# A two-layer hybrid block on one core: the causal mask goes beside the maximum, work moves from VectorE to ScalarE, and the first and last stages are written in another order

## The chip, the core and the metric

The kernel runs on one core of a Trainium2 chip. The core has a matmul engine (TensorE, PE in the profile, with its weight loads as PEld), a vector engine (VectorE, DVE), a scalar engine (ScalarE, ACT), a small general engine (GpSimd, POOL) and SyncE (SP), which issues most of the DMAs. Each engine works through its own list of instructions in order and waits on semaphores of the others. Matmul results land in PSUM; DVE and ACT take them from there to SBUF. The metric is the device time of one execution in microseconds (us); lower is better.

## The reference

512 tokens of width 1024 go through two layers, each a mixing part and a gated feed-forward part, with RMS norms before and after each and a residual sum. Layer A mixes by chunked spatial gating, layer B by attention with forget gates over 12 heads of 64 (the "fox" heads here). Both add four heads of attention over 256 memory rows. Cut to what the change touches:

```
def forgetting_attention(q, k, v, log_f):
    c = jnp.cumsum(log_f, axis=1)
    ...
        logits = jnp.einsum('bthd,bshd->bhts', qi, k).astype(jnp.float32) * scale
        logits = logits + ci[..., :, None] - cT[..., None, :]
        mask = kpos[None, :] <= qpos[:, None]
        logits = jnp.where(mask, logits, -jnp.inf)
        p = jax.nn.softmax(logits, axis=-1).astype(v.dtype)
        return jnp.einsum('bhts,bshd->bthd', p, v)

    # end of each layer
    f = (jax.nn.silu(f @ w_ffn_gate[layer]) * (f @ w_ffn_up[layer])) @ w_ffn_down[layer]
    h = h + rmsnorm(f, ln_ffn_post[layer])
```

where `rmsnorm(x, g)` is `x * rsqrt(mean(x * x) + 1e-6) * g` along the width.

## The kernel before

The state `h` is kept transposed in SBUF: 8 blocks of 128 rows of the width, by 512 tokens (`h`, 128x8x512). Every fp32 operand of a product is cut into two parts, `hi` and `lo` (`split`, L241: ACT casts the high part, DVE subtracts to get the low part), and `mm3` (L193 to L195) makes three matmuls of each product: hi by hi, lo by hi, hi by lo. Weights stream from HBM in pieces of 512 KB through four `raw` buffers (SP issues them) and are split on the way. So PE always has three matmuls for one product, while ACT and DVE split the next weights beside it. The order of the work is that of the code, except that the framework's scheduler may move instructions past each other on each engine; the order listings below show what came out.

**Start (`layer_a`).** `query_weights(m, c0, c1)` loads and splits a piece of the two blocks of query weights, `tokens(k0, k1)` loads blocks of the input into `h` and splits them scaled by the norm's gain (`ahi` L245 on ACT, `alo` L246 on DVE). The first products then run over k, both query blocks for each k, and behind each of the two products of k = 0 stand two matmuls on zeros (`idle`, L88), which only keep PE busy. Then follow the value blocks (`v`), the norm's sums, and the rest of the layer.

**Spatial gating of layer A.** `spatial(g)` makes two PSUM tiles `s` from the ring of three buffers named `lg` (the rings are `mm` and `lg` with three buffers each, `tr` with two). Just before, two tiles `rows` of the same ring are filled, and DVE adds them into `bsp` (L768).

**Fox heads of layer B (`attend`, `FoxHead`, `Softmax`).** For each head there are four blocks of 128 queries, `tb` = 3, 2, 1, 0, that see 512, 384, 256 and 128 keys. `steps` fixes the order of one head: S3, S2, S1, S0 are the logits, N2 and N0 the scalings, T0 to T2 the transposes and V0 to V2 the value products of the head before, and F0 to F4 pieces of other work (key, value and output blocks). One step S (`logits`) makes two matmuls into a PSUM tile `lg` (L504, L505) and a third (L506) that adds the causal mask: -1e30 above the diagonal, as a bf16 128x128 product of `neg` with an identity, `ident_b`. `weigh` then takes the row maximum on DVE (L440, `nmx`) and the exponential on ACT from PSUM into `p` in SBUF, with the row's sum `sm` (L441). `norm` inverts two sums and scales two blocks of `p` on DVE (L448, L450). `turn` transposes `p` on PE (L457) into `tr` and splits it (`pT`), and `values` multiplies it with the values (L525). `value_block` in `layer_b` takes 12 blocks of values, 128x256, out of PSUM on DVE, scaled by the norm (L1247).

**End (`tail_of`, `give`).** The last feed-forward product is made for four blocks of 128 tokens, `tail(0)` to `tail(3)`. Each gives two PSUM tiles `y` of 128x512, which DVE adds to the sums so far (L816); ACT takes the sums of squares (L819), POOL the power -1/2 (L262), and ACT scales the rows by it (L840; in the last block L836 on ACT and L835 on DVE). In the last block the second tile is made in two halves of 256 columns, in one PSUM tile. `give(tb, ...)` transposes the finished rows back, 128x128 at a time (`turned`, L847), and `residual` (L852) multiplies each transposed block with the gain and adds it to `h`, one DVE instruction for each 128x128. Then `h` goes out by DMA (L1369). Between the last product and the last transposes eight matmuls on zeros keep PE busy.

## Time and profile before

| | before |
|---|---|
| median of 3 runs | 1113.27 us (1113.27 to 1113.5) |
| the profiled execution's own time | 1111.68 us |
| its span, first to last instruction | 1110.0 us |
| PE busy | 1100.9 us, 7384 matmuls |
| PEld busy | 999.7 us |
| DVE busy | 895.0 us |
| ACT busy | 667.1 us |
| mean granted clock of PE | 0.999 |

Times are microseconds from the start of the span. In a row of a timeline stand the start, the length, the engine, the line of the kernel, the operation, the tiles written and read, and in brackets how long the engine was idle before and what ended that. Matmuls are pipelined, so their lengths overlap; what one costs is the distance from its start to the next one's start. A row of a table by groups shows count, busy time, mean ns of one, and idle time before them. A row of a table by windows shows the stretch, its length, and the busy time of PE, PEld, DVE, ACT and POOL in it (with counts), the granted clock, the share of the DMA engines, and GB/s. What the profile calls ACTIVATION_READ_ACCUMULATOR is a second instruction, by which ACT writes out a row sum.

### The profile page before, as it was taken

To read this page: it belongs to the slowest core of one execution; us is meant where nothing else is said; L and a number is where in the kernel's file an instruction comes from. 1 tells how busy PE (TensorE), PEld (TensorE's weight loads), DVE (VectorE), ACT (ScalarE), POOL (GpSimd) and SP (SyncE) were. 2 spreads that over 40 slices of the span, in tenths; PEclk is the share of its full clock that TensorE was granted. 3 is DMA by queue.
4 is the path that set the end of the run, shared out by engine and by line. 5 is a ranking of instruction groups with operands and counts; after the bars stand their busy time and mean duration, and the time that the engine had idled before them with its cause. 6 is when DMAs were issued, how large, how long until landed. Compare 5 with 4: busy or idle time off the path is not lost.

```text
span 1110.0 us, 19527 instructions
## 1 busy us (share of the span) xinstructions
PE 1100.9 (99%) x7384; PEld 999.7 (90%) x7385; DVE 895.0 (81%) x1734; ACT 667.1 (60%) x1401; POOL 25.1 (2%) x41
## 2 busy tenths in 40 slices
PE   9999999999999999999999999999999999999998
PEld 6997889999899899998988897889999899899996
DVE  7879659897698598787868889868897698588775
ACT  7776578664366254477647667768665266254453
POOL 0000000000000000001000000000000000000000
PEclk9999999999999999999999999999999999999999
DMA  7521331334135133245222555431234134233222
GB/s 268 159 79 58 113 116 39 115 115 136 55 115 152 56 96 115 79 150 173 77 76 75 155 124 131 129 115 39 77 97 151 58 115 134 58 114 114 77 76 77
DMA packets 63558, 118.13 MB, mean 106 GB/s; under 512 B 5164, under 2 KB 39992, under 8 KB 63464
## 3 DMA queue, kind: packets, MB, share of 16 engines
q1 hardware_dynamic: 62584, 116.05, 34.4%
q8 instruction: 58, 0.95, 0.4%
q0 software_dynamic: 192, 0.52, 0.2%
q10 hardware_dynamic: 688, 0.31, 0.1%
q14 instruction: 36, 0.29, 0.1%
HBM read 104.71 MB, written 2.10 MB: 96 GB/s over the span
## 4 chain that ended last, share of the span: by engine, by line
PE 86%; DVE 3%; ACT 1%; issue 1%; DMA 0%; POOLq 0%; POOL 0%; DVEq 0%; ACTq 0%
PE y L193 10%; PE y L194 10%; PE y L195 10%; PE a L194 5%; PE a L195 5%; PE a L193 5%; PE ps L193 3%; PE ps L194 3%; PE ps L195 3%; PE x L194 3%; PE x L195 3%; PE x L193 3%; PE e L193 3%; PE e L194 3%; PE e L195 3%; PE tr L457 1%
## 5 line engine op out<-in xcount | busy, mean ns | idle before, releaser
L241 ACT CAST whi<-raw 128x512 fp32r<-128x512 f32 x460 | 277.2, 620 | 266.6 <-PE y L195 118.5
L241 DVE TENSOR_TENSOR wlo<-raw,whi 128x512 fp32r<-128x512 f32 x460 | 306.3, 686 | 117.0 <-ACT whi L241 114.6
L193 PE MATMUL y<-whi,fhi 128*128 128x512 f32 (+1 forms) x356 | 139.7, 393 | 0.0
L194 PE MATMUL y<-wlo,fhi 128*128 128x512 f32 (+1 forms) x356 | 139.5, 392 | 0.0
L195 PE MATMUL y<-whi,flo 128*128 128x512 f32 (+1 forms) x356 | 139.1, 391 | 0.0
L194 PE MATMUL x<-xslo,whi 128*128 128x256 f32 x320 | 89.9, 281 | 0.0
L194 PE MATMUL a<-xslo,whi 128*128 128x256 f32 x320 | 89.9, 281 | 0.0
L195 PE MATMUL x<-xshi,wlo 128*128 128x256 f32 x320 | 89.8, 280 | 0.0
L193 PE MATMUL x<-xshi,whi 128*128 128x256 f32 x320 | 89.7, 280 | 0.0
L195 PE MATMUL a<-xshi,wlo 128*128 128x256 f32 x320 | 89.7, 281 | 0.0
L193 PE MATMUL a<-xshi,whi 128*128 128x256 f32 x320 | 89.6, 280 | 0.0
L195 PEld LDWEIGHTS y<-whi,flo 128*128 128x128 f32 x356 | 66.9, 188 | 15.5 <-DVE flo L241 0.2
L193 PEld LDWEIGHTS y<-whi,fhi 128*128 128x128 f32 x356 | 66.9, 188 | 15.1 <-DVE y L816 0.2
L194 PEld LDWEIGHTS y<-wlo,fhi 128*128 128x128 f32 x356 | 66.9, 188 | 14.7 <-DVE wlo L241 0.2
L193 PE MATMUL ps<-xshi,whi 128*128 128x256 f32 (+1 forms) x224 | 68.4, 306 | 0.0
L194 PE MATMUL ps<-xslo,whi 128*128 128x256 f32 (+1 forms) x224 | 66.7, 298 | 0.0
L195 PE MATMUL ps<-xshi,wlo 128*128 128x256 f32 (+1 forms) x224 | 66.4, 298 | 0.0
L193 PEld LDWEIGHTS a<-xshi,whi 128*128 128x128 f32 x320 | 60.3, 189 | 0.4
L194 PEld LDWEIGHTS a<-xslo,whi 128*128 128x128 f32 x320 | 60.2, 188 | 0.3
L193 PEld LDWEIGHTS x<-xshi,whi 128*128 128x128 f32 x320 | 60.3, 188 | 0.0
L195 PEld LDWEIGHTS x<-xshi,wlo 128*128 128x128 f32 x320 | 60.2, 188 | 0.0
L194 PEld LDWEIGHTS x<-xslo,whi 128*128 128x128 f32 x320 | 60.2, 188 | 0.0
(289 smaller groups left out, 3082.1 us busy)
## 6 DMA issues: line engine op xcount, KB each, us to landing
raw<-in_w_gate SPq DMA_DIRECT2D x44, 512.0 KB
raw<-in_w_up SPq DMA_DIRECT2D x44, 512.0 KB
raw<-in_w_down SPq DMA_DIRECT2D x44, 512.0 KB
raw<-in_w_out SPq DMA_DIRECT2D x16, 512.0 KB
raw<-in_w_b_q SPq DMA_DIRECT2D x8, 512.0 KB
raw<-in_w_a_v SPq DMA_DIRECT2D x6, 512.0 KB
raw<-in_w_a_u SPq DMA_DIRECT2D x6, 512.0 KB
raw<-in_w_v SPq DMA_DIRECT2D x6, 512.0 KB
```

The source lines that it names most:

```text
L193: PE.matmul(o, w[0], x[0], start=start, stop=False, skip_group_check=more)
L194: PE.matmul(o, w[0], x[1], start=False, stop=False, skip_group_check=more)
L195: return PE.matmul(o, w[1], x[0], start=False, stop=stop, skip_group_check=more)
L241: last_parts[:] = A.copy(hi, src), (eng or V).tensor_sub(lo, src, hi)
L457: PE.transpose(tr[:, at * P : (at + 1) * P], src, ident)
```

## The change

1. **Mask.** The third matmul and `ident_b` go. `neg` becomes 128x512 in bf16, zero but for its last 128 columns. DVE's maximum becomes one `tensor_tensor_reduce`: it adds the last `n` columns of `neg` to the logits, takes the negative, writes the result to `p` in SBUF and reduces by the minimum to `nmx`. In the listing that is two instructions, named ISA: the operation, and the write of `nmx`. The exponential then works in place on `p`, with scale -1.
2. **Scaling.** For the widest block of each head (`tb` = 3, 512 columns) ACT scales `p` instead of DVE (`by_scalar`).
3. **Values.** ACT takes layer B's 12 value blocks out of PSUM instead of DVE.
4. **Start.** The tokens' blocks 0 to 3 are loaded one by one ahead of the second query block's first half; the second halves come later; the first products run by halves of k, one query block after the other, and the four matmuls on zeros are gone.
5. **Spatial gating.** The two tiles `s` come from the rings `mm` and `lg` in turn.
6. **End.** The last norm's gain is turned to a row on PE, written to HBM (a tile `row`, issued by ACT) in layer A and read back into a `raw` buffer, 128x1024, the same row in every partition, behind `tail(0)`. For the last two blocks of tokens DVE multiplies the sums with the gains ahead of the norm (`gained`), so that the transposed blocks are only added to `h`, 256 or 512 columns at a time. The last block's second half has a PSUM tile of its own. The transposes of block 2 stand behind the last product, and six matmuls on zeros instead of eight behind them.

```diff
-    ident_b = cp.tile([P, P], BF16, name="ident_b")
-    V.tensor_copy(ident_b, ident)
...
-    neg = cp.tile([P, P], BF16, name="neg")
-    V.tensor_copy(neg, neg_f[:, :P])
+    neg = cp.tile([P, T], BF16, name="neg")
+    V.tensor_copy(neg, neg_f)
...
-        def weigh(self, tb, lg, p):
+        def weigh(self, tb, lg, p, mask=None):
...
+            else:
+                V.tensor_tensor_reduce(out=p, in0=lg, in1=mask, scale=-1.0, scalar=-NEG, op0=ALU.add, op1=ALU.min,
+                                       accum_out=self.nmx[:, c])
+                last_exp[0] = A.activation(p, p, AF.Exp, bias=self.nmx[:, c], scale=-1.0, accum_out=self.sm[:, c])
...
-                V.tensor_scalar_mul(self.p[x], self.p[x], self.sm[:, x : x + 1])
+                if x in self.by_scalar:
+                    A.activation(self.p[x], self.p[x], AF.Copy, scale=self.sm[:, x : x + 1])
+                else:
+                    V.tensor_scalar_mul(self.p[x], self.p[x], self.sm[:, x : x + 1])
...
-            PE.matmul(lg[:, :n], qc[:68, c], kc[:68, :n], start=False, stop=False)
-            PE.matmul(lg[:, c], ident_b, neg, start=False, stop=True)
+            PE.matmul(lg[:, :n], qc[:68, c], kc[:68, :n], start=False, stop=True)
...
+    def row_of_gains(block):
+
+        gain_row[0] = dp.tile([KT, P], F32, name="row")
+        o, row = ps("tr", (KT, P), s="gr"), temp("row", (KT, P))
+        PE.transpose(o, gains[:, block * KT : block * KT + KT], ident)
+        A.copy(row, o)
+        nc.scalar.dma_start(gain_row[0], row)
+
+    def spread_gains():
+
+        row = gain_row[0]
+        gain_row[0] = wp.tile([P, D], F32, tag="raw", name=name("raw"), bufs=4)
+        nc.sync.dma_start(gain_row[0], row.rearrange("a b -> (a b)").partition_broadcast(P))
...
         query_weights(0, 0, 512)
-        tokens(0, 1)
-        query_weights(1, 0, 1024)
-        tokens(1, 2)
-        tokens(2, 4)
+        for k in range(4):
+            tokens(k, k + 1)
+        query_weights(1, 0, 512)
         query_weights(0, 512, 1024)
         tokens(4, 6)
         tokens(6, 8)
         last_a = tuple(last_parts)
+        query_weights(1, 512, 1024)
...
-            for k in range(KT):
+            for half in range(0, KT, 4):
                 for o, w in zip(outs, wq):
-                    end = mm3(o, w[k], a[k], k == 0, k == KT - 1)
-                    if k == 0:
-                        idle(2, zero, end)
+                    for k in range(half, half + 4):
+                        mm3(o, w[k], a[k], k == 0, k == KT - 1)
...
-                    o = ps("lg", (P, 2, 2, P), s="s")
+                    o = ps(("mm", "lg")[tp2], (P, 2, 2, P), s="s")
...
+                    if added and not (final and dh):
+                        V.tensor_mul(gained[tb][dh][:, cols], y, gain_row[0][:, 512 * dh + m0 * P : 512 * dh + m1 * P])
...
-                    V.tensor_scalar_mul(ys[tb][1][:, cols], ys[tb][1][:, cols], r[:, c])
-                    A.activation(ys[tb][0][:, cols], ys[tb][0][:, cols], AF.Copy, scale=r[:, c])
+                    y0, y1 = (y[:, cols] for y in gained[tb])
+                    V.scalar_tensor_tensor(out=y1, in0=ys[tb][1][:, cols], scalar=r[:, c],
+                                           in1=gain_row[0][:, 512 + m * P : 512 + (m + 2) * P],
+                                           op0=ALU.mult, op1=ALU.mult)
+                    A.activation(y0, y0, AF.Copy, scale=r[:, c])
...
-                    V.tensor_scalar_mul(vals[j, tk // 2][:, tk % 2, :], o[tk][:, :256], r4b[:, tk : tk + 1])
+                    A.activation(vals[j, tk // 2][:, tk % 2, :], o[tk][:, :256], AF.Copy, scale=r4b[:, tk : tk + 1])
...
+    def give_added(tb, order, tags, queues=(nc.sync,), end=None, held={}):
...
+                for x, k in enumerate(some):
+                    row_turned(gained[tb], k, tr[:, x, :])
+            with behind(held.get(n, ())):
+                V.tensor_add(h[:, k0:k1, c[0] : c[1]], tr, h[:, k0:k1, c[0] : c[1]])
+            queues[n % len(queues)].dma_start(out[:, k0:k1, c[0] : c[1]], h[:, k0:k1, c[0] : c[1]])
...
-    idle(8, zero, end)
-    give(TB - 1, (range(4, 6), range(2), range(6, 8), range(2, 4)), (nc.sync, nc.scalar))
+    give_added(TB - 2, (range(2), range(2, 4), range(4, 8)), ("tr", "tr", "mm"), end=end, held={2: [sums]})
+    idle(6, zero, end)
+    give_added(TB - 1, (range(4, 6), range(2), range(6, 8), range(2, 4)), ("lg", "mm") * 2, (nc.sync, nc.scalar))
```

How the change stands in the lists of the engines is shown at three places. First PE in the middle of a fox head, at S3 (`lg`, from `ka` and `qa`, then `kc` and `qc`), with the transposes T1 of the head before (`tr`) behind it. Before:

```order
L504 MATMUL lg_7758<-ka_7659,qa_7658 128x512
L505 MATMUL lg_7758<-kc_6910,qc_6908 128x512
L506 LDWEIGHTS ident_b
L506 MATMUL lg_7758<-neg,ident_b 128x128
L457 MATMUL tr_7775<-ident,p_7682 128x128
L457 MATMUL tr_7775<-ident,p_7655 128x128
L457 MATMUL tr_7775<-ident,p_7631 128x128 x2
L504 MATMUL lg_7784<-ka_7659,qa_7658 128x384
```

The same place now:

```order
L512 MATMUL lg_7752<-ka_7655,qa_7654 128x512
L513 MATMUL lg_7752<-kc_6912,qc_6910 128x512
L464 MATMUL tr_7768<-ident,p_7677 128x128
L464 MATMUL tr_7768<-ident,p_7651 128x128
L464 MATMUL tr_7768<-ident,p_7628 128x128 x2
L512 MATMUL lg_7777<-ka_7655,qa_7654 128x384
```

The mask's weight load and matmul are gone, 48 times in all; the rest of the heads' work on PE keeps its order but for a few places where neighbours changed.

Second DVE in the same head, from the low part of T0's transposes to the scaling of the two wide blocks (`nmx` is the negative maximum, `p` the weights, `sm` their sums). Before:

```order
L241 TENSOR_TENSOR pT_7751<-tr_7749,pT_7750 128x512
L440 TENSOR_REDUCE nmx_6928<-lg_7758 128x1
L241 TENSOR_TENSOR pT_7777<-tr_7775,pT_7776 128x512
L440 TENSOR_REDUCE nmx_6928<-lg_7784 128x1
L241 TENSOR_TENSOR wlo_7895<-q_6121,whi_7894 128x512
L440 TENSOR_REDUCE nmx_6928<-lg_7801 128x1
L448 RECIPROCAL sm_6929<-sm_6929 128x2
L241 TENSOR_TENSOR pT_7813<-tr_7811,pT_7812 128x256
L450 TENSOR_SCALAR p_7762<-p_7762,sm_6929 128x512
L450 TENSOR_SCALAR p_7788<-p_7788,sm_6929 128x384
```

The same place now:

```order
L239 TENSOR_TENSOR pT_7745<-tr_7743,pT_7744 128x512
L443 ISA p_7755,nmx_6930<-lg_7752,neg 128x512
L443 ISA nmx_6930 128x1
L239 TENSOR_TENSOR pT_7770<-tr_7768,pT_7769 128x512
L443 ISA p_7780,nmx_6930<-lg_7777,neg 128x384
L443 ISA nmx_6930 128x1
L239 TENSOR_TENSOR wlo_7884<-q_6123,whi_7883 128x512
L443 ISA p_7796,nmx_6930<-lg_7793,neg 128x256
L443 ISA nmx_6930 128x1
L452 RECIPROCAL sm_6931<-sm_6931 128x2
L239 TENSOR_TENSOR pT_7804<-tr_7802,pT_7803 128x256
L457 TENSOR_SCALAR p_7780<-p_7780,sm_6931 128x384
```

Each maximum has become two instructions, the second of them one column wide; the scaling of 512 columns has left DVE, and on ACT it now stands between the exponential of 256 columns and that of 128.

Third DVE at the very end, from the sum of the last block's first half-tile on (`y` the sums, `yt` the transposed blocks, `two` and `v` the sums of squares, `r` the factor of the norm). Before:

```order
L816 TENSOR_TENSOR y_9720<-y_13392,y_9720 128x256
L852 SCALAR_TENSOR_TENSOR h<-yt_13440,gains,h 128x128 x2
L821 SCALAR_TENSOR_TENSOR v_13182<-ss_13181,two_13375,eps_13177 128x1
L852 SCALAR_TENSOR_TENSOR h<-yt_13440,gains,h 128x128
L835 TENSOR_SCALAR y_9720<-y_9720,r_13183 128x256 x2
L852 SCALAR_TENSOR_TENSOR h<-yt_13440,gains,h 128x128
L852 SCALAR_TENSOR_TENSOR h<-yt_13459,gains,h 128x128 x2
L852 SCALAR_TENSOR_TENSOR h<-yt_13465,gains,h 128x128 x2
L852 SCALAR_TENSOR_TENSOR h<-yt_13471,gains,h 128x128 x2
L852 SCALAR_TENSOR_TENSOR h<-yt_13477,gains,h 128x128 x2
```

The same place now:

```order
L841 TENSOR_TENSOR y_9674<-y_13372,y_9674 128x256
L1403 TENSOR_TENSOR h<-yt_13394,h 128x2x128
L1403 TENSOR_TENSOR h<-yt_13399,h 128x2x128
L848 SCALAR_TENSOR_TENSOR v_13136<-ss_13135,two_13337,eps_13131 128x1
L1403 TENSOR_TENSOR h<-yt_13404,h 128x4x128
L863 SCALAR_TENSOR_TENSOR yg_13336<-y_9674,r_13137,raw_13217 128x256 x2
L1403 TENSOR_TENSOR h<-yt_13423,h 128x2x128
L1403 TENSOR_TENSOR h<-yt_13418,h 128x2x128
L1403 TENSOR_TENSOR h<-yt_13428,h 128x2x128
L1403 TENSOR_TENSOR h<-yt_13433,h 128x2x128
```

Behind the last two products with `r` stand four sums of 256 columns where eight of 128 stood; ahead of `v` stand two sums of block 2.

More of the change, by code (lines that the diff above doesn't have):

```diff
@@ L430, in hybrid @@
     class Softmax:
+        by_scalar = ()
         def __init__(self):
@@ L511, in logits @@
             at = 384 if tb == 0 else 0
-            self.weigh(tb, lg[:, :n], (self.beside if tb == 0 else self.room)[:, at : at + n])
+            self.weigh(tb, lg[:, :n], (self.beside if tb == 0 else self.room)[:, at : at + n], neg[:, T - n :])
         def transpose(self, b):
@@ L803, in tail @@
             c = slice(tb, tb + 1)
+            added = last and tb >= TB - 2
             final = last and tb == TB - 1
+            if added:
+                gained[tb] = [plain("yg") for _ in range(2)]
             two = small("two", 1) if final else None
@@ L820, in tail @@
                     if n == len(at) - 1:
-                        V.scalar_tensor_tensor(out=v[:, c], in0=one, scalar=run, in1=eps[:, c] if eps is not None else rms_eps,
+                        total = V.scalar_tensor_tensor(out=v[:, c], in0=one, scalar=run, in1=eps[:, c] if eps is not None else rms_eps,
                                                op0=ALU.add, op1=ALU.add)
@@ L834, in tail @@
                     cols = slice(m * P, (m + 2) * P)
-                    V.tensor_scalar_mul(ys[tb][1][:, cols], ys[tb][1][:, cols], r[:, c])
-                    A.activation(ys[tb][0][:, cols], ys[tb][0][:, cols], AF.Copy, scale=r[:, c])
-                return end
+                    y0, y1 = (y[:, cols] for y in gained[tb])
[3 more added lines that the diff above has]
+                    A.activation(y0, y0, AF.Copy, scale=r[:, c])
+                return end, total
             with urgent(tb):
-                for y in ys[tb]:
+                for y in gained[tb] if added else ys[tb]:
                     A.activation(y, y, AF.Copy, scale=r[:, c])
+            return end, total
         return tail, ys
@@ L846, in turned, with row_turned @@
         for n, tb in enumerate(tbs):
-            PE.transpose(out[:, n * P : (n + 1) * P], ys[tb][k // 4][:, k % 4 * P : (k % 4 + 1) * P], ident)
+            row_turned(ys[tb], k, out[:, n * P : (n + 1) * P])
+    def row_turned(y, k, out):
+        PE.transpose(out, y[k // 4][:, k % 4 * P : (k % 4 + 1) * P], ident)
     def residual(o, k, cols, post):
@@ L1357, in hybrid @@
         tail, ys = feed_forward(1, phase, xp)
+    def give_added(tb, order, tags, queues=(nc.sync,), end=None, held={}):
+        c = (tb * P, (tb + 1) * P)
+        for n, some in enumerate(order):
+            tr = ps(tags[n], (P, len(some), P), s="yt")
+            k0, k1 = some[0], some[-1] + 1
+            with behind([end] if end else ()):
+                for x, k in enumerate(some):
[3 more added lines that the diff above has]
+            queues[n % len(queues)].dma_start(out[:, k0:k1, c[0] : c[1]], h[:, k0:k1, c[0] : c[1]])
     def give(tb, order, queues=(nc.sync,)):
```

26 lines of the change are left out of this document (16 added, 10 removed).

## The prediction

> **What bounds the kernel.** I read the page first, then the windows by stage, then the waits and the timeline where they point.
>
> ```profile
> PE 1100.9 (99%) x7384; PEld 999.7 (90%) x7385; DVE 895.0 (81%) x1734; ACT 667.1 (60%) x1401; POOL 25.1 (2%) x41
> PE 86%; DVE 3%; ACT 1%; issue 1%; DMA 0%; POOLq 0%; POOL 0%; DVEq 0%; ACTq 0%
> 0.00:20.00 20.00, 17.84 (x69) 11.19 (x70) 14.59 (x28) 15.31 (x26) 1.32 (x7) 1.00 0.90 333
> 590.00:730.00 140.00, 139.41 (x867) 118.50 (x866) 120.20 (x285) 99.10 (x247) 0.00 (x0) 1.00 0.47 122
> 660.00:700.00 40.00, 39.41 (x238) 32.32 (x237) 37.57 (x89) 29.97 (x78) 0.00 (x0) 1.00 0.59 143
> 1096.00:1110.00 14.00, 8.99 (x55) 6.46 (x54) 8.05 (x28) 3.99 (x10) 0.93 (x2) 0.90 0.40 113
> ```
>
> PE is busy 99% of the span, and the chain that ended last is PE for 86%. So time is won in two ways: by work that leaves PE, and where PE waits, at the two ends (17.84 of 20 us, 8.99 of 14 us) and in single places. In layer B's attention (590 to 730 us) DVE is busy 86%, and 94% from 660 to 700 us, where PE begins to lose time (39.41 of 40). There a cost on DVE can reach PE. The feed-forward parts keep their instructions and their order, so I count nothing there.
>
> **The mask on PE.** The timeline of PE at two masks, and one weight load:
>
> ```profile
> 634.45 0.23 PE L506 MATMUL lg<-neg,ident_b 128*128 128x128 bf16 x1
> 634.49 0.48 PE L193 MATMUL k<-shi,whi 128*128 128x512 f32 x1
> 634.81 0.39 PE L194 MATMUL k<-slo,whi 128*128 128x512 f32 x1
> 635.04 0.39 PE L195 MATMUL k<-shi,wlo 128*128 128x512 f32 x1
> 634.44 0.10 PEld L506 LDWEIGHTS <-ident_b 128*128 128x128 bf16 x1 [0.15 <-issue]
> 642.23 0.60 PE L457 MATMUL tr<-ident,p 128*128 128x128 f32 x4
> 642.58 0.48 PE L504 MATMUL lg<-ka,qa 128*128 128x512 f32 x1
> 642.90 0.40 PE L505 MATMUL lg<-kc,qc 68*128 68x512 f32 x1
> 643.21 0.61 PE L457 MATMUL tr<-ident,p 128*128 128x128 f32 x4
> 643.57 0.42 PE L504 MATMUL lg<-ka,qa 128*128 128x384 f32 x1
> ```
>
> A mask takes 0.04 us from its start to the next start (634.45 to 634.49). But its weights load only when the matmul before has ended (634.44), and the next weights only behind it, so the next matmul of 512 columns takes 0.32 us (634.49 to 634.81) where its neighbour takes 0.23. Together 0.13 us. In front of four transposes it is less: from 642.90 to 643.57 are 0.67 us, and without the mask 0.23 for the 512 columns and 0.35 for the transposes (642.23 to 642.58), so 0.09. Twelve heads have four masks each, two with 0.13 and two with 0.09: 12 x 0.44 = **5.3 us** that leave PE.
>
> [...]
>
> **What DVE and ACT take on in that stage.** The groups of the stage, and two of ACT from elsewhere:
>
> ```profile
> L440 DVE TENSOR_REDUCE nmx<-lg 128x1 f32<-128x512 f32 x12 | 8.2, 685 | 2.3 <-PE lg L506 2.3
> L440 DVE TENSOR_REDUCE nmx<-lg 128x1 f32<-128x128 f32 x12 | 3.4, 283 | 0.2
> L241 DVE TENSOR_TENSOR pT<-tr,pT 128x512 fp32r<-128x512 f32 x32 | 21.4, 683 | 1.8 <-ACT pT L241 1.8
> L448 DVE RECIPROCAL sm<-sm 128x2 f32<-128x2 f32 x32 | 5.1, 160 | 3.2 <-ACT p L441 2.2 <-ACT mp L441 0.8
> L450 DVE TENSOR_SCALAR p<-p,sm 128x512 f32<-128x512 f32 x12 | 5.8, 481 | 0.1
> L1247 DVE TENSOR_SCALAR vf<-v,r 128x256 f32<-128x256 f32 x12 | 5.8, 481 | 2.4 <-PE v L195 2.1
> L618 ACT ACTIVATE vg<-v,r 128x256 f32<-128x256 f32 x12 | 5.6, 473 | 6.9 <-PE v L195 4.5 <-POOL r L262 2.4
> L840 ACT ACTIVATE y<-y,r 128x512 f32<-128x512 f32 x30 | 20.1, 716 | 9.3 <-POOL r L262 9.0
> ```
>
> *DVE.* The trace shows no reduction with a mask. The nearest operation with two inputs, one in PSUM, is the low part `pT`: 683 ns, the same as the 685 of the plain maximum. I take the same price; bounds are the plain maximum and twice its time per column. The write of `nmx` is new. The smallest DVE row of the stage, the reciprocal of two columns, takes 160 ns and overlaps with its neighbours; I take 0.1 us each, between 0 and 0.16, so 48 x 0.1 = +4.8 us. Scaling and values leave: 12 x 0.481 + 12 x 0.481 = -11.5 us. The cast of the wider `neg` is a few tenths at the start. In sum DVE loses about 7 us.
>
> *ACT.* It gains 12 x 0.716 + 12 x 0.473 = 14.3 us, and the exponential now reads SBUF, for at most a few hundredths more each, so some 16 us on 99.1. That is 115 of about 136 us, 85%: cover is there on average, and PE need not wait. Where ACT is late, the wide block's scaling stands ahead of the exponential of 128 columns, which the next head's first transposes wait for: up to 0.7 us a head.
>
> [...] If only the sum of work counted, the wide scaling would cost 12 x 0.235 = 2.8 us; I count nothing, since ACT has the room.
>
> **Where PE already waits for the softmax.** The scaling of the two narrow blocks, then the transposes that need it (an early head is 640.63 against the 642.23 above), the wait for `lg`, and another stall:
>
> ```profile
> 640.63 0.54 DVE L450 TENSOR_SCALAR p<-p,sm 128x256 f32<-128x256 f32 x2
> 693.24 0.54 DVE L450 TENSOR_SCALAR p<-p,sm 128x256 f32<-128x256 f32 x2
> 693.84 0.33 PE L457 MATMUL tr<-ident,p 128*128 128x128 f32 x1 [0.24 <-DVE p L450]
> PEld lg L504 <- ACT p L441: 0.9, 2, 0.5
> 98.33 0.36 PE L735 MATMUL s<-ws,vhi 128*128 128x256 f32 x1 [1.13 <-DVE bsp L768]
> ```
>
> The early head has 1.1 us to spare (641.17 to 642.23); the late one has none (693.78 to 693.84). About half of the heads, 655 to 705 us, are of the second kind. There a faster PE only waits longer, and the path from the last logits to the scaled block is longer by the write of `nmx`. I give back 0.35 us in each of six heads: 2.1 us. On the other side `lg` is now free once DVE has read it, not when ACT has: the 0.9 us of waiting for ACT goes. So the stage gives -5.3 - 0.9 + 2.1 = **-4.1 us**, between -6.2 (nothing given back) and 0 (DVE or ACT sets the pace).
>
> **Spatial gating.** PE waits 1.13 us for `bsp`, because the second `s` needs the first `rows` buffer of the same ring. With the first `s` in `mm`, whose buffers are older, the second takes the third `lg` buffer. I take **-1.1 us**; next to be late is DVE's work behind it, with a gate block of PE in between, so at most half comes back. The turn of the gains adds **+0.1** on PE there; ACT's DMA issue and copy lie beside PE's gate blocks.
>
> **Start.**
>
> ```profile
> 1.25 3.97 PE L88 MATMUL idle<-zeros 128*128 128x512 bf16 x10 [1.25 <-DVE zeros L80]
> 5.56 0.50 PE L193 MATMUL ps<-ahi,whi 128*128 128x512 f32 x1 [0.34 <-ACT ahi L245]
> 6.92 0.60 PE L88 MATMUL idle<-zeros 128*128 128x512 bf16 x2
> 19.25 0.28 PE L193 MATMUL v<-whi,ahi 128*128 128x256 f32 x1
> ```
>
> The 48 first matmuls need 48 x 0.232 = 11.1 us and get 13.7 (5.56 to 19.25), so 2.6 us are waits and zeros. The DMAs move 333 GB/s (the first window), so a block of 256 KB takes 0.79 us. By the old order k = 1 comes behind two blocks and a 512 KB piece; by the new one every 0.79 us a block arrives, where PE needs 0.70 for its three matmuls. The first low part still costs 0.55 us, the arrivals some 0.1 each, and the low parts on DVE (one behind each block) a few tenths; the half of the second query block comes fifth instead of third on SP, about when PE asks for it. That leaves some 1.3 of the 2.6 us. The norm's sums behind it, on DVE, do not come as much earlier. **-1.0 us**, between 0 and -1.5.
>
> **End.**
>
> ```profile
> 1082.44 1.28 DVE L241 TENSOR_TENSOR wlo<-raw,whi 128x512 fp32r<-128x512 f32 x2
> 1091.48 0.68 DVE L816 TENSOR_TENSOR y<-y,y 128x512 f32<-128x512 f32 x1
> 1098.95 0.71 PE L847 MATMUL yt<-ident,y 128*128 128x128 f32 x5
> 1099.63 0.39 PE L193 MATMUL y<-whi,fhi 128*128 128x256 f32 x1
> 1101.37 0.42 DVE L816 TENSOR_TENSOR y<-y,y 128x256 f32<-128x256 f32 x1 [0.54 <-PE y L195]
> 1103.24 0.61 DVE L835 TENSOR_SCALAR y<-y,r 128x256 f32<-128x256 f32 x2 [0.40 <-POOL r L262]
> 1103.77 2.75 DVE L852 SCALAR_TENSOR_TENSOR h<-yt,gains,h 128x128 f32<-128x128 f32 x9
> ```
>
> Five transposes stand between the last two pieces of the product (0.68 us); they go behind them, so `y`, its square and `v` come 0.68 us earlier. Two sums of block 2 now stand ahead of `v` on DVE; they push it back by some 0.1. Then nine sums at 0.305 us, eight of them the last block's (2.4 us), become four of 256 columns. A DVE sum of that width took 0.42 us alone (1101.37), some 0.35 in a row: 1.4 us. The product with the gains is a little longer than the plain scaling, 0.1 us. In sum -0.68 + 0.1 - 1.0 + 0.1 = **-1.5 us**, between -0.8 and -1.8; the last DMA leaves that much earlier. The read-back of the gains stands last on SP ahead of the output's DMAs, and needs a `raw` buffer that the last split of weights (1082.44) frees by 1084 us at the latest. 512 KB at the 113 GB/s of the last window take 4.6 us, to about 1089; the first product with it comes behind the sum of block 2, at 1092. If it is late, DVE stands, and `y` behind it: the price is the delay itself.
>
> **The sum.** -4.1 - 1.1 + 0.1 - 1.0 - 1.5 = -7.6 us. The profiled execution took 1111.68 us, 1.68 around a span of 1110.0, and would take 1104.1. It lies 1.6 us under the median of the runs; against 1113.27 the sum gives **1105.7 us**, 0.68% less. About 0.2% (2.2 us) is what a measurement of this kernel tells from no change, so the border is 1111.0.
>
> **The rivals.**
> - *PE gets all of it.* The six late heads are held by DVE's load, which falls, so nothing is given back: the stage gives -6.2, the sum is -9.7, 1103.6 us. For it: DVE loses some 7 us. Against it: 693.84, where the path and not the load is late.
> - *The softmax sets the pace.* ACT's added 16 us or the writes of `nmx` make the attention as long as before; only the other places count: 1113.27 - 3.5 = 1109.8. For it: DVE at 94% from 660 to 700 us. Against it: DVE gets lighter, and early heads have 1.1 us to spare.
> - *The reduction with a mask runs at half rate.* From 283 to 685 ns for 384 columns are 1.05 ns a column; the 12 x 1280 columns again are 16 us on DVE. With the upper price of the writes DVE has 120.2 - 11.5 + 7.7 + 16.1 = 132.5 us of work; at the 94% that it reached, that is 141 us for a stage of 140: 1110.8, no difference that can be measured. [...]
> - *Slower.* If beyond that each of the 96 new instructions runs alone, without the overlap of some 0.08 us that rows of DVE have, DVE has 140 us of work, at 94% 149 for the stage: +9 - 3.5, 1118.8. It decides from 135 us of DVE work on (143.5 x 0.94), where the stage has eaten the other gains.
> - *PE's clock falls at the start.* The zeros kept PE busy, and the first ten of them ran at 0.40 us each (1.25 to 5.2) where later ones of that width take 0.23. One stretch of 4 us at that rate costs 1.7 us: 1107.4. In the windows the clock is 1.00, with waits of 0.5 us between matmuls, and the new order has no longer ones.
>
> **How the numbers follow.** Forecast 0.54, clock 0.05 (both within 1103.5 to 1108.5), all of it 0.18, the softmax sets the pace 0.14, half rate 0.06, slower 0.03. Two in ten may be left out: the range is 1102.0 to 1110.3, which takes in the first rival and the second and leaves out the last two and the tails. Faster is all but half rate, slower and a little of the second rival: 0.90; same 0.07; slower 0.03.
>
> **What would show it.** The mask's rows gone and the 512-column matmul behind the logits at 0.23 us; ISA rows near 685 and 283 ns, with second rows under 0.16; PE's waits for `p` (L457 before) in 655 to 705 us, under 2 us in sum, and none for `lg`; no wait for `bsp`; the first `v` matmul near 18.2 us; four sums at the end, and the last DMA issue 1.5 us nearer to the last product. Wrong would make me ISA rows over 1 us, PE waiting for ACT in the attention, or a wait for the gains' row at 1092 us.

## The result and the profile after

The changed kernel took 1106.73 us (median of 6 runs, 1106.27 to 1107.84), the kernel before 1113.13 us (6 runs): a ratio of 0.9946, with a 95% interval of 0.9933 to 0.9958. In a second comparison (5 runs against 9) it took 1106.08 us against 1111.85, a ratio of 0.9943 (0.993 to 0.9955). The forecast was 1105.7 us, that is a ratio of 0.9932, so the direction and the range held. The gain was 6.4 us in the first comparison and 5.8 in the second, where the sum has 7.6.

The page and the windows of the changed kernel (PE, weight loads, DVE, ACT, POOL, clock, DMA share, GB/s, as before):

```profile
PE 1096.5 (99%) x7332; PEld 998.5 (90%) x7332; DVE 887.5 (80%) x1751; ACT 679.6 (62%) x1426; POOL 25.2 (2%) x41
PE 93%; ACT 3%; DVE 2%; issue 1%; DMA 0%; SPq 0%; POOLq 0%; POOL 0%; DVEq 0%; ACTq 0%
```

```profile
0.00:20.00 20.00, 18.35 (x69) 11.73 (x70) 14.32 (x27) 14.94 (x26) 1.32 (x7) 1.00 0.90 326
590.00:730.00 140.00, 138.76 (x828) 119.32 (x828) 115.83 (x316) 112.28 (x273) 0.00 (x0) 1.00 0.47 125
660.00:700.00 40.00, 39.06 (x223) 32.75 (x222) 36.43 (x106) 34.13 (x86) 0.00 (x0) 1.00 0.59 150
```

PE is still 99% busy and has more of the chain that ended last (93% instead of 86%). In the attention DVE fell from 120.20 to 115.83 us of 140 and ACT rose from 99.10 to 112.28. PE's own idle time in that window grew, from 0.59 to 1.24 us: part of what the mask left was turned into waits.

Where the time went is read best from the time between two matmuls that both kernels have. Each kernel was profiled twice; the columns give both executions, and the differences are those of the means.

| stretch, on PE where not said | before | changed | difference | in the sum |
|---|---|---|---|---|
| start to the first v matmul | 19.25, 19.69 | 18.76, 18.22 | -0.98 | -1.0 |
| to the first s (spatial gating) | 77.33, 77.38 | 77.57, 77.57 | +0.22 | 0 |
| to the last s | 37.36, 37.35 | 36.12, 36.12 | -1.24 | -1.0 |
| to the first memory logits of layer B | 440.81, 440.44 | 441.34, 441.15 | +0.62 | 0 |
| to the last product of the mixed heads | 175.96, 175.94 | 173.50, 173.39 | -2.51 | -4.1 |
| to the last matmul of 512 columns | 346.58, 346.61 | 345.47, 345.47 | -1.13 | 0 |
| to DVE's last sum (its end) | 9.24, 9.23 | 7.71, 7.70 | -1.53 | -1.5 |
| to the end of the span | 3.4, 3.5 | 3.9, 3.9 | +0.4 | 0 |
| span | 1110.0, 1110.1 | 1104.4, 1103.5 | -6.1 | -7.6 |

The attention is the stretch in which the sum was wrong, by 1.6 us; the end's transfers took back 0.4; two stretches on which nothing was counted moved by half a microsecond and by one.

The groups of the attention in the changed kernel, first those of L443 on DVE from 590 to 730 us, the reduction with the mask and its second row, the write of `nmx`; then those on ACT:

| L443 on DVE | count | busy, us | mean, ns | idle before, us |
|---|---|---|---|---|
| reduction, 128x512 | 12 | 8.2 | 686 | 3.3, for `lg` from PE |
| reduction, 128x128 | 12 | 3.4 | 282 | 0.6, for `lg` from PE |
| write of `nmx`, 128x1 | 48 | 4.0 | 83 | 0.0 |

```profile
L445 ACT ACTIVATE p<-p,nmx 128x512 f32<-128x512 f32 x12 | 8.7, 726 | 2.3 <-DVE nmx L443 2.3
L455 ACT ACTIVATE p<-p,sm 128x512 f32<-128x512 f32 x12 | 8.6, 715 | 0.0
...
L1281 ACT ACTIVATE vf<-v,r 128x256 f32<-128x256 f32 x8 | 3.8, 470 | 2.5 <-PE v L193 2.4
```

The reduction with the mask takes 686 and 282 ns, the plain maximum took 685 and 283; its second row takes 83 ns. These prices were forecast, and so were those on ACT (715 and 470 ns). So the instructions cost what the sum said. What was late, and what a mask had really cost PE, was not what it said. PE's waits of the whole span (engine, tile and line waited for; us in total, times, longest):

```profile
PE o L532 <- ACT pT L239: 0.5, 1, 0.5
...
PE mo L493 <- DVE pT L239: 0.2, 1, 0.2
PE tr L464 <- DVE p L457: 0.2, 1, 0.2
```

No wait for `bsp` is left, and none for `lg`; nor does DVE wait for the gains' row at the end. New is a wait for `pT` from ACT, the sign that the prediction named as one against it.

### The profile page after: what moved, and what is told of

Its sections match the earlier page's. It is cut to its first block, busy times and chain, and to the rows that moved or that the text cites. A ratio compares the mean times of both kernels' runs of the same rounds, so it can differ in the third digit from the quotient of the medians.

```text
span 1104.4 us, 19436 instructions
## 1 busy us (share of the span) xinstructions
PE 1096.5 (99%) x7332; PEld 998.5 (90%) x7332; DVE 887.5 (80%) x1751; ACT 679.6 (62%) x1426; POOL 25.2 (2%) x41
## 4 chain that ended last, share of the span: by engine, by line
PE 93%; ACT 3%; DVE 2%; issue 1%; DMA 0%; SPq 0%; POOLq 0%; POOL 0%; DVEq 0%; ACTq 0%
PE y L191 10%; PE y L192 10%; PE y L193 10%; PE a L191 5%; PE a L193 5%; PE a L192 5%; PE ps L191 4%; PE ps L192 4%; PE ps L193 4%; PE e L191 3%; PE e L193 3%; PE e L192 3%; PE x L193 3%; PE x L191 3%; PE x L192 3%; PE v L191 2%
## 5 line engine op out<-in xcount | busy, mean ns | idle before, releaser
L193 PEld LDWEIGHTS a<-xshi,wlo 128*128 128x128 f32 x320 | 60.2, 188 | 0.0
```

The lines of the kernel that those rows point to most:

```text
L193: return PE.matmul(o, w[1], x[0], start=False, stop=stop, skip_group_check=more)
```

## The experiments

All are changes of the changed kernel, in one place each, unless said otherwise. The attention is measured as in the table above, from the first memory logits of layer B to the last product of the mixed heads: before 175.95 us, changed 173.45 us (means of two).

**The two moves to ScalarE, undone one by one and together.** Without `by_scalar` VectorE scales all four blocks.

```diff
     class FoxHead(Softmax):
-        by_scalar = (3,)
```

> The changed kernel, but VectorE scales the widest block of weights, as before (12 x 0.48 us back on DVE, 12 x 0.715 off ACT). Theory A, ACT has become the late engine of layer B's attention (its casts of pT stand behind its own scaling and exponentials, and PE waits 1.4 us for pT at its weight loads): the waits for pT by ACT between 680 and 700 us go, the time falls by 0.5 to 1.5 us to 1105.2 to 1106.2. Theory B, the path through DVE sets the late heads (the prediction's reason for giving back): with 5.8 us more on DVE the waits for p grow and the time rises by 0.5 to 1.5 us, to 1107.2 to 1108.2. Neither touches the wait of 0.7 us for pT of the memory heads at 597 us.

Measured: 1108.52 us, a ratio of 0.9968 (0.9956 to 0.9981), so slower than the changed kernel (0.9946; the two intervals just touch); attention 175.55 us. PE's waits in it, from 590 to 735 us:

```profile
PE lg L511 <- DMA ka<-whi: 1.2, 1, 1.2
PE tr L464 <- DVE p L457: 0.6, 1, 0.6
...
```

Theory A falls. Part of the loss is B's wait for `p`, but the largest wait is one that no theory named: the logits of a head wait for the copies of its split keys, which are DMAs issued by SP. SP took 2.36 us to issue two of them there (from 684.32 us) and 1.25 for the same two in the changed kernel; why is not shown. The attention was 2.1 us longer in the profile; see below why up to one of them may belong to the execution.

The value blocks back on DVE:

```diff
-                    A.activation(vals[j, tk // 2][:, tk % 2, :], o[tk][:, :256], AF.Copy, scale=r4b[:, tk : tk + 1])
+                    V.tensor_scalar_mul(vals[j, tk // 2][:, tk % 2, :], o[tk][:, :256], r4b[:, tk : tk + 1])
```

> The changed kernel, but VectorE takes layer B's value blocks out of PSUM, as before (12 x 0.48 us on DVE instead of 12 x 0.47 on ACT). Theory C, the order on ACT: with the blocks on ACT the first cast of pT of the memory heads stands behind a table load of 1.28 us, and PE waits at 597 us; with them on DVE the cast stands ahead of the load again, the loss of 0.9 us between 593 and 598 us goes, and the time falls to about 1105.8. Rival: the same tables are loaded in the same place, the wait at 597 stays, and the change is worth nothing or, by more DVE work, costs up to 0.5 us: 1106.7 to 1107.2.

Measured: 1106.37 us, ratio 0.9945 (0.9931 to 0.9958); attention 172.66 us, 0.8 less than the changed kernel. Theory C is right about the place. ACT's timeline there, in the changed kernel and then with the blocks on DVE:

```profile
592.15 1.28 ACT L1298 ACT_TABLE_LOAD   x1
593.44 0.24 ACT L1298 ACTIVATE l<-w 128x48 f32<-128x48 f32 x1
593.59 0.60 ACT L239 CAST whi<-q 128x512 fp32r<-128x512 f32 x1
594.21 1.28 ACT L441 ACT_TABLE_LOAD   x1
595.51 0.47 ACT L441 ACTIVATE mp<-mlg,nmx 128x256 f32<-128x256 f32 x1
595.88 0.19 ACT L441 ACTIVATION_READ_ACCUMULATOR mp<-mlg,nmx 128x1 f32 x1
595.97 1.06 ACT L239 CAST pT<-tr 128x512 fp32r<-128x512 f32 x2
```

```profile
594.41 0.24 ACT L1298 ACTIVATE l<-w 128x48 f32<-128x48 f32 x1
594.56 0.57 ACT L239 CAST pT<-tr 128x512 fp32r<-128x512 f32 x1
595.15 1.28 ACT L441 ACT_TABLE_LOAD   x1
```

With the value blocks on ACT, the scheduler put the first cast of `pT` behind a table load of 1.28 us and an exponential; without them it stands ahead, as it did in the kernel before. PE pays for it in the changed kernel here:

```profile
596.60 0.50 PE L493 MATMUL mo<-pT,memv 128*128 128x512 f32 x1
597.33 0.51 PE L493 MATMUL mo<-pT,memv 128*128 128x512 f32 x1 [0.23 <-DVE pT L239]
```

The second matmul starts 0.73 us after the first where 0.23 is its spacing. Against the kernel before, PE is 0.94 us ahead at 590 us and 0.08 at 600, so the place costs 0.9 us in sum; with the blocks on DVE it costs nothing. Yet the time did not follow: 0.5 us came back between the attention and the last product (346.0 instead of 345.5 us, with instructions that the edit leaves alone).

Both moves undone:

> The changed kernel with both moves to ScalarE undone; the mask with the maximum, the start, the spatial buffers and the end stay. If ACT is the cause of what is missing in the attention (theories A and C together) it is the fastest of the four: 1104.6 to 1105.4, with PE's waits in the attention back to near those of before. If DVE is (theory B), DVE works some 127 us of the 140 of the stage and the time is 1107.5 to 1109.

Measured: 1106.99 us, ratio 0.9958 (0.9945 to 0.9971); attention 174.09 us. So it isn't the fastest, and A and C together do not hold: of the two moves, the wide block on ACT is a gain in the attention (172.66 against 174.09 with the values on DVE), the values on ACT a loss at one place.

**The mask back on PE.**

```diff
-            PE.matmul(lg[:, :n], qc[:68, c], kc[:68, :n], start=False, stop=True)
+            PE.matmul(lg[:, :n], qc[:68, c], kc[:68, :n], start=False, stop=False)
+            PE.matmul(lg[:, c], ident_b, neg[:, T - P :], start=False, stop=True)
...
-            self.weigh(tb, lg[:, :n], (self.beside if tb == 0 else self.room)[:, at : at + n], neg[:, T - n :])
+            self.weigh(tb, lg[:, :n], (self.beside if tb == 0 else self.room)[:, at : at + n])
```

> The changed kernel with the mask added by 48 matmuls again and the plain maximum; both moves to ScalarE stay. If the mask was worth its 5.3 us of PE and the waits stand by themselves: 1106.7 + 5.3 - 0.5 (DVE without the 48 writes) = 1111.5. If PE's waits only fill what the mask left (the softmax sets the pace): 1107 to 1109.

Measured: 1110.84 us (11 runs), ratio 0.9987 (0.9979 to 0.9996); attention 177.60 us, 4.2 more than the changed kernel and 1.7 more than the kernel before. The time lies near the first of the two cases. Neither part alone gives what both give: the two moves to ScalarE with the mask on PE make the attention 1.7 us longer than before (0.9 of it by 600 us, the place above), the mask's removal without the moves makes it 1.9 us shorter (both_on_dve), and with the wide scaling on ACT 3.3 (values_on_dve). So without the mask's removal there is no gain, and the wide scaling adds to it. What the mask cost PE is read from an early head, in which nothing waits: from its first transposes to the product behind its last `o`, before and changed:

```profile
623.13 0.60 PE L457 MATMUL tr<-ident,p 128*128 128x128 f32 x4
623.48 0.48 PE L504 MATMUL lg<-ka,qa 128*128 128x512 f32 x1
623.80 0.40 PE L505 MATMUL lg<-kc,qc 68*128 68x512 f32 x1
624.04 0.23 PE L506 MATMUL lg<-neg,ident_b 128*128 128x128 bf16 x1
624.11 0.60 PE L457 MATMUL tr<-ident,p 128*128 128x128 f32 x4
...
624.73 0.33 PE L505 MATMUL lg<-kc,qc 68*128 68x384 f32 x1
624.91 0.23 PE L506 MATMUL lg<-neg,ident_b 128*128 128x128 bf16 x1
624.95 0.48 PE L193 MATMUL k<-shi,whi 128*128 128x512 f32 x1
625.27 0.40 PE L194 MATMUL k<-slo,whi 128*128 128x512 f32 x1
...
629.62 0.45 PE L193 MATMUL k<-shi,whi 128*128 128x512 f32 x1
```

```profile
622.65 0.60 PE L464 MATMUL tr<-ident,p 128*128 128x128 f32 x4
623.01 0.48 PE L512 MATMUL lg<-ka,qa 128*128 128x512 f32 x1
623.32 0.40 PE L513 MATMUL lg<-kc,qc 68*128 68x512 f32 x1
623.56 0.60 PE L464 MATMUL tr<-ident,p 128*128 128x128 f32 x4
...
624.17 0.34 PE L513 MATMUL lg<-kc,qc 68*128 68x384 f32 x1
624.36 0.40 PE L191 MATMUL k<-shi,whi 128*128 128x512 f32 x1
624.59 0.40 PE L192 MATMUL k<-slo,whi 128*128 128x512 f32 x1
...
628.81 0.45 PE L191 MATMUL k<-shi,whi 128*128 128x512 f32 x1
```

6.49 and 6.16 us: four masks are worth 0.33 us in this head, not 0.44, and twelve such heads 4.0 us, not 5.3. In front of transposes a mask costs 0.07 (623.80 to 624.11 against 623.32 to 623.56), in front of a product of 512 columns 0.12 (624.73 to 625.27 against 624.17 to 624.59); only one of the head's four masks stands in front of such a product.

**GpSimd takes the wide block** (value blocks on DVE):

```diff
-                    A.activation(self.p[x], self.p[x], AF.Copy, scale=self.sm[:, x : x + 1])
+                    G.tensor_scalar_mul(self.p[x], self.p[x], self.sm[:, x : x + 1])
```

> The changed kernel with layer B's value blocks taken out by VectorE (as in values_on_dve) and the widest block of weights scaled by GpSimd, which does nothing else in the attention. Theory F: what is left of PE's waits there (2.5 us of them from 660 to 700 us in values_on_dve, for pT by ACT and by DVE) is ACT's and DVE's load in the late heads; with 12 x 0.715 us off ACT and nothing on DVE these waits fall by 1 to 1.5 us and the time by as much, to about 1105 us by a before of 1112. Rival: GpSimd takes over 2 us for a block of 512 columns, or slows DVE beside it, the scaled block becomes what the first transposes wait for, and the time rises by 1 us or more per 0.1 us that each head is late: 1107 to 1112.

Measured: 1107.61 us, ratio 0.9952 (0.9938 to 0.9966); attention 173.64 us, 1.0 more than with ACT. The rival holds in its second form, a slower DVE; by their intervals the times alone do not tell the two kernels apart. Its group on POOL, then a DVE group beside it with one of its twelve instructions, and the same group in values_on_dve:

```profile
L455 POOL TENSOR_SCALAR p<-p,sm 128x512 f32<-128x512 f32 x12 | 21.5, 1793 | 118.9 <-DVE sm L452 77.0 <-PE o L532 19.8 <-DVE nmx L443 14.4
```

```profile
L457 DVE TENSOR_SCALAR p<-p,sm 128x384 f32<-128x384 f32 x12 | 6.6, 548 | 0.1
...
627.75 0.85 DVE L457 TENSOR_SCALAR p<-p,sm 128x384 f32<-128x384 f32 x1
```

```profile
L457 DVE TENSOR_SCALAR p<-p,sm 128x384 f32<-128x384 f32 x12 | 5.0, 417 | 0.1
```

POOL takes 1.79 us where ACT takes 0.72, and slows DVE beside it: 548 instead of 417 ns for the same block. That is a mean of two kinds: four of the twelve took 0.76 to 0.85 us, eight the usual 0.41 to 0.42. The late heads' transposes then wait for `p` from DVE (1.7 us in four waits), not for POOL's block.

**GpSimd makes the low parts of the values** (values_on_dve, with `G` as the engine of the subtraction in `values()`):

> values_on_dve, and GpSimd instead of VectorE makes the low parts of each head's values (12 subtractions of 256 columns, 0.42 us each on DVE; they are made a head ahead, so their own duration should not matter). Theory G, what is left of PE's waits in the late heads is DVE's load: with 5 us off DVE the waits from 660 to 705 us (2.5 us in values_on_dve) fall by 0.5 to 1 us, ratio 0.9935. Rival: GpSimd slows DVE's operations on SBUF beside it, as in wide_scale_on_pool (548 instead of 417 ns at 384 columns), and the time stays or rises by up to 1 us: 0.9941 to 0.995.

Measured: 1105.97 us, ratio 0.9945 (0.9931 to 0.9959); attention 173.38 us. DVE had 117.43 us of work from 590 to 730 us instead of 119.60, and the time did not fall. The order on ACT moved once more: the two casts of `pT` stand behind the table load again, as in the changed kernel, and that place cost 1.0 us; the rest of the attention gained 0.2. Theory G isn't borne out: less load on DVE didn't shorten the late heads by what it took off.

**The three other places.** The old start:

```diff
-        for k in range(4):
-            tokens(k, k + 1)
-        query_weights(1, 0, 512)
+        tokens(0, 1)
+        query_weights(1, 0, 1024)
+        tokens(1, 2)
+        tokens(2, 4)
...
-        query_weights(1, 512, 1024)
...
-            for half in range(0, KT, 4):
-                for o, w in zip(outs, wq):
-                    for k in range(half, half + 4):
-                        mm3(o, w[k], a[k], k == 0, k == KT - 1)
+            for k in range(KT):
+                for o, w in zip(outs, wq):
+                    end = mm3(o, w[k], a[k], k == 0, k == KT - 1)
+                    if k == 0:
+                        idle(2, zero, end)
```

> The changed kernel with the old start (order of the first loads, order of the query products, two zeros matmuls behind the first product). Theory D (the prediction's): the order of arrival is worth 1.0 us, the first v matmul comes near 19.3 us and the time is 1 us above the changed kernel's. Theory E: when the first blocks land differs from execution to execution by more than the order is worth (the first v matmul came between 18.3 and 20.2 us in five profiles with the new order); then it lies in that stretch here too and the time is within 0.5 us of the changed kernel's.

Measured: 1107.10 us, ratio 0.9953 (0.9941 to 0.9966). The first v matmul of this kernel, and the earliest and the latest of the eleven profiles with the new order:

```profile
19.85 0.28 PE L191 MATMUL v<-whi,ahi 128*128 128x256 f32 x1
```

```profile
18.22 0.28 PE L191 MATMUL v<-whi,ahi 128*128 128x256 f32 x1
```

```profile
20.19 0.28 PE L193 MATMUL v<-whi,ahi 128*128 128x256 f32 x1
```

Both theories hold a part. Three profiles with the old order have 19.25, 19.69 and 19.85 (mean 19.60), eleven with the new one 18.22 to 20.19 (mean 18.92): 0.7 us, of which 0.2 are lost again by the first s (77.57 instead of 77.35 us behind it). One profile can't tell it. The latest of the eleven, mask_back_on_pe, is late for another reason: its granted clock was halved for 3.4 us, and products of 512 columns came 0.43 us apart there instead of 0.23. Its window:

```profile
8.30:11.70 3.40, 3.40 (x8) 2.72 (x9) 3.22 (x7) 2.67 (x5) 0.00 (x0) 0.50 1.03 408
```

The ten others have 18.22 to 19.52 (mean 18.79). Farther on, too, old_start goes with the kernel before: from the last s to layer B's first memory logits it took 440.51 us (before 440.44 and 440.81; the eleven with the new start 441.12 to 441.68), and from the last product of the mixed heads to the last matmul of 512 columns 346.49 (before 346.6; the eleven 345.43 to 346.19). So the two shifts on which nothing was counted come with the start's edit, by this one profile, though other edits move the second of them too (346.0 with the values on DVE); how is not shown.

The old end (the nine sums with a scalar, the five transposes ahead of the last piece, no row of gains; the last lines of the change's diff taken back):

> The changed kernel with the old end (gains applied behind the transposes by nine sums with a scalar, five transposes between the last two pieces of the product) and without the row of gains. By the changed kernel's trace the end is worth 1.1 us of span (from the product at 1090 us to the end): the time is 1.1 us above the changed kernel's, DVE's last sum 1.5 us later against the products, and the stretch from DVE's last sum to the end 3.5 us instead of 3.9. By the prediction's sum it is 1.5 us.

Measured: 1109.05 us (7 runs), ratio 0.997 (0.9959 to 0.9981). DVE's last sums here, and in the changed kernel:

```profile
1099.29 2.76 DVE L857 SCALAR_TENSOR_TENSOR h<-yt,gains,h 128x128 f32<-128x128 f32 x9
```

```profile
1099.06 1.42 DVE L1403 TENSOR_TENSOR h<-yt,h 128x256 f32<-128x256 f32 x4 [0.15 <-PE yt L881]
```

From the last matmul of 512 columns to the end of these sums it takes 9.26 us with the old end and 7.71 with the new one: 1.55 us. The stretch behind it was 4.7 us in this profile, where the kernel before had 3.4 and 3.5, so the span alone would overrate the end. In that stretch lies one packet of the instruction queue (q8, 0.02 MB), and the output's last transfers trickle at 8 to 23 GB/s; the first profiles of the kernel before and of the changed kernel have no packet of that queue there. That it held them up is likely, not tested.

Both s in one ring:

```diff
-                    o = ps(("mm", "lg")[tp2], (P, 2, 2, P), s="s")
+                    o = ps("lg", (P, 2, 2, P), s="s")
```

> The changed kernel with both spatial blocks s in the same ring of PSUM buffers again. By the prediction PE waits 1.1 us for bsp near 97 us again, and all behind it comes 1.1 to 1.3 us later. The rival, that DVE is late there anyway and the ring only names the wait: 0.5 us or less.

Measured: one run of 1108.87 us; from the first to the last s 37.40 us instead of 36.12, so 1.28 us, and the wait is there:

```profile
98.79 0.35 PE L757 MATMUL s<-ws,vhi 128*128 128x256 f32 x1 [1.10 <-DVE bsp L791]
```

The prediction is right here, the rival is not. This run shows something else too. On every engine its instructions stand in the same order as the changed kernel's, yet its attention took 174.46 us, 1.0 more. One cast on ACT, first here, then in the changed kernel:

```profile
637.66 0.62 ACT L239 CAST whi<-q 128x512 fp32r<-128x512 f32 x1 [1.74 <-DMA qa<-whi]
```

```profile
634.86 0.62 ACT L239 CAST whi<-q 128x512 fp32r<-128x512 f32 x1 [0.78 <-DMA qa<-whi]
```

The cast needs a buffer that a copy of an earlier head's queries still reads, and it waited 0.96 us longer for that; old_start has the same wait at 1.9 us and 174.52 us of attention. So about 1 us of the attention hangs on when SP's copies land, and a difference of that size between two single profiles isn't the edit's. The 0.8 us of values_on_dve is: it lies at 597 us, ahead of that place, and came twice.

**Both once more, and the kernel before.**

> The changed kernel itself, once more, beside the two below. If the profiles' differences between executions come from when transfers land (start, keys of the attention), the two profiles of this kernel differ by up to 1.5 us at the first v matmul and by up to 1 us from 630 to 660 us, and by nothing at 597 us (the loss of 0.9 us is there again), at the second spatial block (no wait) and in DVE's last sums. If the attention's course is the order's alone, they differ by under 0.2 us there. Time: ratio 0.9946 to the kernel before, as first measured.

> The changed kernel with layer B's value blocks taken out by VectorE, once more, as the candidate for the best version. By theory C it lies 0.8 us under the changed kernel of the same call (ratio 0.9939 where that has 0.9946); by the rival (the time is taken back elsewhere) the two are the same within 0.3 us.

> The kernel before, profiled a second time: how far its course moves from execution to execution. The wait of 1.1 to 1.2 us for bsp, the five transposes between the pieces of the last product and DVE's last sum against them should be the same; the first v matmul may move by up to 1.5 us, the attention by up to 1 us.

Measured: 1106.08 us (ratio 0.9943) and 1106.12 us (ratio 0.9941, 0.9928 to 0.9955); before 1111.8 us. The two versions are the same within what can be measured, so the rival of theory C holds for the time. Attention: 173.39, 172.66 and 175.94 us, each within 0.11 us of the same kernel's first profile. From one execution of the same kernel to the next the course of the attention hardly moves; the start does (18.76 and 18.22 us). No version beat the changed kernel by an amount that was measured.

## Why the prediction was right, and where it was not

*The mask on PE* was mis-sized: 4.0 us left PE, not 5.3. The prediction took 0.13 us where a long matmul follows a mask and 0.09 before transposes, and counted two of each in a head: 0.44 us, where 0.33 was measured. The prices were near (0.12 and 0.07); the count was wrong, since a product of 512 columns follows only one of that head's four masks, and 10 of all 48. In the mean of the head's four places a mask was worth 0.08 us.

*DVE and ACT* were right instruction by instruction: the reduction at the plain maximum's price, 83 ns for the write (0.1 assumed), 715 and 470 ns on ACT, 13.2 us more on ACT from 590 to 730 us (16 assumed for the stage; that window holds 8 of the 12 value blocks). The half rate of the third rival was a supposition of the author's; no run shows it, and 686 and 282 ns refute it. The wide block took 0.72 us on ACT where it took 0.48 on DVE in the kernel before. Still the attention was 1.4 us shorter with it on ACT (both_on_dve against values_on_dve, timed 0.9958 and 0.9945; the intervals overlap, and a part may be the copies of SP).

*The softmax's waits.* The sum gave back 2.1 us and took 0.9 for `lg`, 1.2 net. The values_on_dve profiles, without the loss at 597 us, have 3.3 of the mask's 4.0 us: 0.7 went back, so the mechanism fits and the size was somewhat too large. No run separates the part that went back from the wait for `lg` that went. What failed is the step that ACT "has the room", for which nothing was counted. ACT had it on average, but its order is the scheduler's, and the added work turned a cast behind a table load: 0.8 to 0.9 us that no step of the prediction had. In the late heads one `o` also waited 0.5 us for ACT's cast of `pT`. So the attention gave 4.0 - 0.7 - 0.8 = 2.5 us, not 4.1.

*Spatial gating*: -1.0 forecast with the turn of the gains, -1.24 measured, by the wait that was named. *Start*: -1.0 forecast, -0.7 at the first v matmul in the mean (-0.8 without the profile of the halved clock) and -0.5 by the first s; the forecast named 18.2 us for it, which is the early end of the executions. *End*: the work is 1.53 us earlier (1.5 forecast; four sums in 1.42 us against 1.4 forecast). But the four last pieces now come closer together, and from DVE's last sum to the end of the span takes 0.4 us more; the prediction let the end follow the last DMA issue unchanged. The time is in the transfers: the output's last packet ends 1.5 us behind DVE's last sum in both profiles of the kernel before and 1.9 in all eleven with the new end. That the closer pieces are the reason is argued, not shown.

*Nothing was counted* for the rest, by the reason that it keeps its instructions and their order. It moved all the same: +0.6 us between the gating and layer B, -1.1 behind the attention. By old_start's one profile both come with the start's edit, so what the start is worth in the whole stays open. That the two made up for a third of the attention's shortfall is luck and no merit of the prediction.

Of the rivals, "PE gets all of it" and "the softmax sets the pace" are both refuted by the attention's -2.5 us, and the DVE rows exclude the two slow ones. The fall of the clock at the start is not refuted: the changed kernel's first profile has 1.00 from 0 to 20 us, but mask_back_on_pe, with the same start, has 0.50 for 3.4 us.

## What to carry to other kernels

Price a small instruction that is taken out of a stream by the length of a whole repeat without waits, from its first to its last matmul, and not by the sum of gaps picked beside it; where the two differ, count the places one by one (here 0.33 us a head against 0.44). When work is moved to an engine whose order a scheduler makes, compare that engine's order around its table loads and the casts that PE waits for, since the average of its free time says nothing about them (here 0.9 us of PE's time, by one cast behind a table load of 1.28 us). Judge an edit worth under 1 us by the stretch it touches, between two matmuls that both kernels have, and only after the same kernel has been profiled twice.

## What the runs showed of the hardware

- GpSimd beside VectorE slowed it in wide_scale_on_pool, but not all of it: while POOL scaled a block of 512 columns, 1.79 us in the mean, four of twelve scalings of 384 columns on DVE took 0.76 to 0.85 us instead of 0.42, the others the usual time, and one subtraction of 512 columns took 1.03 instead of 0.67 us. That subtraction ended inside the 2.08 us that the profile gives POOL's instruction, which began 0.7 us ahead of it (spans on POOL are rough), so it did not wait for POOL's end. What holds DVE up is not shown.
- An exponential of 512 columns took 726 ns from SBUF where the one from PSUM took 692 in the kernel before; the maximum with the mask, 686 ns for 512 columns, cost nothing over the plain one's 685 but its second row of 83 ns.
- The spacing of long runs of equal matmuls moved by build, not by execution, in the three kernels that were profiled twice: from the last product of the mixed heads to the last matmul of 512 columns it took 346.6 us in both profiles of the kernel before, 345.5 in both of the changed one, 346.0 and 346.1 with the values on DVE. These are fractions of a nanosecond for each of some 2400 matmuls, with no wait in the profile. What sets them stays open.
- The granted clock was 0.50 from 8.3 to 11.7 us in the profile of mask_back_on_pe, and products of 512 columns then came 0.43 us apart instead of 0.23; it was 1.00 in the first 20 us of the first profiles of the kernel before and of the changed kernel.
